# RWKV's A products in tied groups of quadrants, the key's norm as a scale of tokens, and other numbers of streamed products in a hybrid decoder step

## The chip, the cores and the metric

One NeuronCore of a Trainium2 chip runs the whole program. The metric is the device time of one execution in microseconds; lower is better. Engines are named as in the profile: PE is TensorE's matmul, PEld its weight load, DVE VectorE, ACT ScalarE, POOL GpSimd, SP SyncE, which issues most DMAs.

## What is computed

One layer of a hybrid decoder for 512 prompt tokens and 8 x 8 sampled tokens (576 in all), model width 1024, in fp32. RWKV-7 time mixing and differential attention run as two branches on the same normed input, are merged by gates, and a squared-ReLU MLP and a final norm follow. The change is in the RWKV branch. For each of 8 heads of 64, with a per-token decay, a, k, v and r:

```
kk = hs((k * lp['k_k']).astype(f32))
kk = kk / jnp.maximum(jnp.linalg.norm(kk, axis=-1, keepdims=True), 1e-12)
k = k.astype(f32) * (1.0 + (a - 1.0) * lp['k_a'].astype(f32))
S, y = rwkv7_scan(S0, hs(r), hs(decay), hs(k), hs(v), -kk, kk * hs(a))
```

where each step of the scan is

```
sa = jnp.einsum('bhij,bhj->bhi', S, a_t)
S = S * w_t[:, :, None, :] + sa[..., None] * b_t[:, :, None, :] + v_t[..., None] * k_t[:, :, None, :]
return S, jnp.einsum('bhij,bhj->bhi', S, r_t)
```

## The kernel before

The scan is done in chunks of 64 tokens: eight of the prompt, and a ninth that holds the sampled tokens. Activations lie with features on the 128 partitions, so that one tile holds two heads, one on each half; a "head pair" hp is such a tile, four in all (0 to 3), and `halves` names the two halves (par 0 and 1).

`rwkv(hp)` is a generator in stages; `run(...)` near the end calls them in an order that is written out by hand.

- Stage 0 (L753 to L838) makes the operands. The key's squares are summed over each head (pn) and raised to -1/2 on GpSimd (nr, L760). A wide copy on GpSimd repeats each norm over 64 columns (nb, L763), five transposes (pk, pks) turn it round, and VectorE multiplies it into the key (kk, in the buffer sq). The decay's running sum is a scan over tokens (cum, L777), of which ScalarE takes three exponentials (pe, pinv, pm). KB holds a·kk and the scaled key, ST holds -kk and r, each with its decay. The two heads are made by separate instructions on 64 partitions each: in KB head 0 has a·kk first and head 1 second, and ST has one tile per head whose other half is set to zero by GpSimd (L819).
- The A products (pA, L834 on) multiply KB, as weights, by ST for each head and chunk: 18 products of 128 rows and 128 columns a head pair. Because the other half of ST is zero, the sum over 128 rows is that of one head; the 128 outputs are its products with both parts of KB. VectorE masks the results into ABR (own part) and into the free half of ST (other part).
- Stage 1 transposes v (pV, copied into SVU) and KB (pK, copied into KBt) and multiplies the state by ST's ninth chunk (pI).
- Stage 2 solves a triangular system a chunk, in 32x32 blocks: DT is taken from ABR (ScalarE, four pieces), masked into Y and DM, and four rounds of pW, ScalarE's W, pZ, VectorE's update of X and a transpose follow; then pWc and pC fill TT.
- `chain(pr)` walks through the chunks for two head pairs at once with small products (pch), and later stages finish the output.

**What orders the work.** The program is written in Tile, which sorts each engine's instructions by priority and by their readiness as it reckons it; the order is fixed when the program is built, and each engine's queue runs in order. The large products (attention's and RWKV's projections `ps_z`, gates `ps_g`, `ps_brb`) are generators in the list `waiting`. `take(n)` puts out the next n of their matmuls at low priority, so that they fill TensorE between the small dependent steps; `fill(n)` does so behind the last matmul; `blocks` takes nine behind each step of the solve. These are the streamed products: 128 x 128 weights by 288 or 296 columns, in three terms of split fp32. The numbers after each `run` say how many are spent there. PSUM has three rotating banks for this work (`bank`, pool psw), and one more, `tbank`.

`with tc.issue_after(x)` keeps the instructions of a block behind x on its engine. In `chain` a group of products on different quadrants is tied that way to its first one.

Of the kernel before, what the change touches and what calls it, by code (L numbers as in the profile page):

```python
# [41 lines left out]
def tile_hybrid_step(ctx, tc, xT, xsT, ktab, vtab, s0T, ptab, w_in, vecs, w2a2, g2, lamv,  # L42
# [273 lines left out]
    ts(hw0, v(V_W0, 8), 0.5, MUL, 0.0, ADD, GE)  # L316
    ka2 = rc.tile([P, 8], F32, name="ka2")
# [424 lines left out]
    def rwkv(hp):  # L742
# [12 lines left out]
        for t, o in enumerate(toks):  # L755
# [4 lines left out]
        GE.tensor_tensor(out=nr, in0=nr, in1=mhalf[:, :10], op=ALU.pow)  # L760

        nb = rt.tile([P, 5, P], F32, tag="G", name=f"nb{hp}", bufs=3)
        own["nb"] = GE.tensor_copy(out=nb.rearrange("p t (a d) -> p (t a) d", a=2),  # L763
                       in_=nr.rearrange("p (a o) -> p a o", o=1).broadcast_to([P, 10, 64]))
# [16 lines left out]
        VE.tensor_copy(out=pc[:, 0:8], in_=pe[:, 63:NPR:64])  # L781
        VE.tensor_copy(out=pc[:, 8:16], in_=pe[:, NPR + 7::8])
# [5 lines left out]

        kk = sq
# [5 lines left out]
        pk = pks  # L795
        stt(kk[:, NPR:], k[:, NPR:], v(V_KK + hp), pk[:, 64:P], MUL, MUL)

# [14 lines left out]
        stt(aa, aa, 1.0, kk, ADD, MUL)  # L812
        ST = []
        for par, rows in halves:
            stt(KB[rows, :, par], ch(aa)[rows], 0.5, ch(pinv)[rows], MUL, MUL)
            tt(KB[rows, :, 1 - par], ch(k2)[rows], ch(pinv)[rows], MUL)
            st = rb_.tile([P, NCH, 2, 64], F32, tag=f"ST{par}", name=f"ST{par}_{hp}")
            with tc.issue_after(own["nb"].ins) if hp == 0 else nullcontext():
                GE.memset(st[64 - 64 * par:128 - 64 * par], 0.0)  # L819
            stt(st[rows, :, 0], ch(kk)[rows], -1.0, ch(pm)[rows], MUL, MUL)  # L820
            tt(st[rows, :, 1], ch(r)[rows], ch(pe)[rows], MUL)
            ST.append(st)
# [4 lines left out]
        for par in range(2):  # L827
            rows = slice(64 * par, 64 * par + 64)
            oth = slice(64 - 64 * par, 128 - 64 * par)
            for c0, cn, mk in ((0, 4, C_M), (4, 4, C_M), (8, 1, C_MS)):  # L830
                pA = bank(f"pA{hp}{par}{c0}")
                for i in range(cn):
                    mm(pA[:, i * P:(i + 1) * P], KBc[c0 + i], ST[par][:, c0 + i])
                pAv = pA[:, :cn * P].rearrange("p (c w) -> p c w", c=cn)  # L834
                f2 = lambda a: a[:, c0:c0 + cn].rearrange("p c a t -> p c (a t)")
# [690 lines left out]
```

## Time and profile before

| | |
|---|---|
| time, median of 3 runs | 991.74 us (990.62 to 992.3) |
| the profiled execution | 993.35 us |
| its span | 991.6 us |
| TensorE busy | 964.5 us |
| VectorE busy | 694.3 us |
| ScalarE busy | 495.1 us |
| GpSimd busy | 91.0 us |

Times in a timeline count from the span's start. A row of a timeline gives the start, the length, the engine, the line and what is written from what; `x18` means that 18 such records follow each other, and the length goes from the first start to the last end. A matmul of fp32 appears as two records, one of split fp32 (`ps_...`) as one. Ends of matmuls are modelled: records overlap, and the distance of starts is what one costs. Most operations go through helpers, so that a line such as L61 or L72 says only which helper; rows are told apart by tile.

### The profile page before, as it was taken

The page shows a single profiled execution, that of the slowest core. Times are in us where ns is not written, and L with a number is a line of the kernel's source. Part 1 is how long each engine was busy: PE and PEld are TensorE (multiplying, and loading weights), DVE is VectorE, ACT ScalarE, POOL GpSimd, SP SyncE. Part 2 cuts the span into 40 slices and gives each one's busy share as a digit, 9 for nine tenths or more (in the row PEclk, how much of TensorE's full clock was granted, in tenths as well). Part 3 has the DMA queues.
Part 4 walks back from the last instruction along what each step waited for, and adds up shares of the span by engine and source line. Part 5 has one row for each costly group of instructions (what it writes and reads, how often), then busy time and mean ns, then how long its engine had stood idle before and what let it go on. Part 6 is the DMA issues. An engine that isn't in the chain of part 4 may idle for free.

```text
span 991.6 us, 24377 instructions
## 1 busy us (share of the span) xinstructions
PE 964.5 (97%) x9996; PEld 913.4 (92%) x9996; DVE 694.3 (70%) x1459; ACT 495.1 (50%) x1084; POOL 91.0 (9%) x171
## 2 busy tenths in 40 slices
PE   8999999999999998999999999999999999999996
PEld 8999989898986898988889999999999999999996
DVE  6698566874945779445688898966666666666744
ACT  6576455354344455443344767444444444444732
POOL 2611100401003230001200000000000000000001
PEclk9999999999999999999999999999999999999998
DMA  7322673221112215222377642222222222221402
GB/s 266 128 76 76 210 220 117 80 59 52 44 63 74 79 62 161 79 70 100 121 234 223 209 132 97 87 94 86 86 86 86 85 86 86 86 87 42 136 3 95
DMA packets 50832, 105.73 MB, mean 107 GB/s; under 512 B 6066, under 2 KB 8114, under 8 KB 50594
## 3 DMA queue, kind: packets, MB, share of 16 engines
q1 hardware_dynamic: 47442, 96.95, 30.4%
q0 software_dynamic: 1648, 5.35, 1.5%
q8 instruction: 78, 1.28, 0.6%
q10 hardware_dynamic: 1632, 1.89, 0.5%
q14 instruction: 32, 0.26, 0.1%
HBM read 89.38 MB, written 14.78 MB: 105 GB/s over the span
## 4 chain that ended last, share of the span: by engine, by line
PE 83%; DVE 6%; issue 6%; ACT 3%; POOL 1%; DMA 0%; SPq 0%; DVEq 0%; POOLq 0%; ACTq 0%
PE ps_dn L72 21%; PE ps_z L72 8%; PE ps_g L72 7%; PE ux L1250 5%; PE ua L1250 5%; PE ps_wo L72 4%; PE ps_brb L72 3%; PE ps_k L72 3%; PE ub L1250 3%; PE ud L1250 3%; PE ps_bra L72 3%; PE uc L1250 3%; PE pch L1010 2%; PE ps_q L72 2%; PE ps_v L72 2%
## 5 line engine op out<-in xcount | busy, mean ns | idle before, releaser
L72 PE MATMUL ps_dn<-q,hi_dn 128*128 128x288 f32 x768 | 154.7, 296 | 0.0
L72 PEld LDWEIGHTS ps_dn<-q,hi_dn 128*128 128x128 f32 x768 | 122.9, 188 | 1.4
L72 PE MATMUL ps_dn<-q,lo_dn 128*128 128x288 f32 x384 | 113.3, 295 | 0.0
L72 PE MATMUL ps_g<-xl,hi_g 128*128 128x288 f32 x256 | 79.7, 311 | 0.0
L72 PE MATMUL ps_g<-xh,lo_g 128*128 128x288 f32 x256 | 79.2, 309 | 0.0
L72 PE MATMUL ps_g<-xh,hi_g 128*128 128x288 f32 x256 | 78.5, 307 | 0.0
L72 PEld LDWEIGHTS ps_dn<-q,lo_dn 128*128 128x128 f32 x384 | 72.2, 188 | 0.0
L72 PE MATMUL ps_z<-xh,lo_z 128*128 128x288 f32 (+1 forms) x224 | 69.2, 310 | 0.0
L72 PE MATMUL ps_z<-xh,hi_z 128*128 128x288 f32 (+1 forms) x224 | 68.0, 303 | 0.0
L72 PE MATMUL ps_z<-xl,hi_z 128*128 128x288 f32 (+1 forms) x224 | 66.9, 299 | 0.0
L61 DVE TENSOR_TENSOR ya<-ya,ps_dn 128x288 f32<-128x288 f32 x96 | 43.3, 451 | 27.6 <-PE ps_dn L72 27.5
L58 ACT ACTIVATE hi_dn<-raw_dn 128x512 fp32r<-128x512 f32 x48 | 30.1, 628 | 56.2 <-PE ps_dn L72 56.1
L58 ACT ACTIVATE c<-c 128x288 f32<-128x288 f32 x112 | 48.8, 440 | 9.4 <-DVE c L61 7.7
L1250 PE MATMUL ux<-h_t,hi 128*128 128x288 f32 x256 | 52.4, 297 | 0.0
L1250 PE MATMUL ua<-h_b,hi 128*128 128x288 f32 x256 | 52.2, 296 | 0.0
L72 PEld LDWEIGHTS ps_g<-xl,hi_g 128*128 128x128 f32 x256 | 48.9, 191 | 1.5
L72 PEld LDWEIGHTS ps_g<-xh,lo_g 128*128 128x128 f32 x256 | 49.0, 191 | 1.3
L72 PEld LDWEIGHTS ps_g<-xh,hi_g 128*128 128x128 f32 x256 | 48.8, 191 | 1.0
L58 ACT ACTIVATE hi<-a 128x1024 fp32r<-128x1024 f32 (+1 forms) x32 | 27.1, 846 | 43.1 <-PE ps_dn L72 34.9
L61 DVE TENSOR_TENSOR lo<-s,hi 128x1024 fp32r<-128x1024 f32 x32 | 39.2, 1224 | 10.4 <-ACT hi L58 10.3
L72 PE MATMUL ps_dn<-q,w 128*128 128x320 f32 (+1 forms) x336 | 46.3, 298 | 0.0
L72 PEld LDWEIGHTS ps_dn<-q,w 128*128 128x128 f32 x336 | 45.3, 190 | 0.1
(391 smaller groups left out, 2789.1 us busy)
## 6 DMA issues: line engine op xcount, KB each, us to landing
a<-in_w_up_dram SPq DMA_DIRECT2D x32, 512.0 KB, 3.3
raw_dn<-in_w_down_dram SPq DMA_DIRECT2D x64, 256.0 KB, 2.8
raw_g<-in_w_in_dram SPq DMA_DIRECT2D x32, 256.0 KB, 3.0
raw_z<-in_w_in_dram SPq DMA_DIRECT2D x28, 256.0 KB, 3.1
gt_d<-gg SPq DMA_DIRECT2D x16, 288.0 KB, 2.3
g<-gt_d SPq DMA_DIRECT2D x16, 288.0 KB, 3.6
kp<-in_ktab_dram SPq DMA_DIRECT2D x16, 256.0 KB, 4.0
vp<-in_vtab_dram SPq DMA_DIRECT2D x16, 256.0 KB, 3.4
```

The lines of the kernel that those rows point to most:

```text
L58: ring["act"] = AE.activation(out=out, in_=in_, func=func, **kw)
L61: ins = (eng or VE).tensor_tensor(out=out, in0=a, in1=b, op=op)
L72: ring["mm"] = PE.matmul(out=out, lhsT=lhsT, rhs=rhs, start=start, stop=stop)
L1010: ring["mm"] = PE.matmul(out=ps[rows, e], lhsT=lhs, rhs=rhs, start=first and e == 1, stop=True, skip_group_check=True)
L1250: ring["mm"] = PE.matmul(out=ps[:, :288], lhsT=l[:, k], rhs=hb[blk][:, h, k], start=start and i == 0, stop=i == 11, skip_group_check=skip)
```

## The change

- The key's norm is no longer multiplied into the key. KB and ST hold the key without it (with k_k and its sign in `hkk` and `nkk`), and the inverse square of the norm, by VectorE's reciprocal, is brought by six small GpSimd copies into `dn`, one number for each token and head with tokens on partitions. It scales DT ahead of the solve and X behind it. nb, its transposes and kk go.
- KB and ST are made by one instruction for both heads, with a·kk first in both. ST of head 1 is a ScalarE copy of half of head 0's tile; the zeros go.
- Each A product becomes four of 64 rows and 64 columns (`quarter`), one on each quadrant: par chooses the rows, d the part of KB and with it the output's half. d = 0 and d = 1 go to different banks. They are tied in two groups a head pair: chunks 0 to 3 and 8, then chunks 4 to 7. VectorE takes d = 0 for both heads in one instruction into ABR.
- pK is copied to KBt in three pieces a bank instead of one, since the halves must be put back as `chain` wants them.
- The two small columns of decays, pc, come from ScalarE instead of VectorE; pbn uses `tbank`.
- The numbers of `take` around the stages differ; the streamed products are the same in all.

```
+    nkk = rc.tile([P, 4], F32, name="nkk")
+    ts(nkk, v(V_KK, 4), -1.0, MUL, 0.0, ADD, GE)
+    hkk = rc.tile([P, 4], F32, name="hkk")
+    ts(hkk, v(V_KK, 4), 0.5, MUL, 0.0, ADD, GE)
...
         ts(nr, pn[:, 0:10], 1e-24, MAX)
-        GE.tensor_tensor(out=nr, in0=nr, in1=mhalf[:, :10], op=ALU.pow)
-        nb = rt.tile([P, 5, P], F32, tag="G", name=f"nb{hp}", bufs=3)
-        own["nb"] = GE.tensor_copy(out=nb.rearrange("p t (a d) -> p (t a) d", a=2),
-                       in_=nr.rearrange("p (a o) -> p a o", o=1).broadcast_to([P, 10, 64]))
+        VE.reciprocal(out=nr, in_=nr)
+        dn = stat.tile([P, NCH], F32, tag="dn", name=f"dn{hp}", bufs=4)
+        n2 = nr.rearrange("p (t a) -> p t a", a=2)
+        for par, rows in halves:
+            GE.tensor_copy(out=dn[rows, 0:8:2], in_=n2[0:64, 0:4, par])
+            GE.tensor_copy(out=dn[rows, 1:8:2], in_=n2[64:128, 0:4, par])
+            own["nb"] = GE.tensor_copy(out=dn[rows, 8:9], in_=n2[64:128, 4:5, par])
...
-        VE.tensor_copy(out=pc[:, 0:8], in_=pe[:, 63:NPR:64])
-        VE.tensor_copy(out=pc[:, 8:16], in_=pe[:, NPR + 7::8])
+        act(pc[:, 0:8], cum[:, 63:NPR:64], AF.Exp, scale=-KAPPA)
+        act(pc[:, 8:16], cum[:, NPR + 7::8], AF.Exp, scale=-KAPPA)
...
-        pk, pks = bank(f"pk{hp}"), bank(f"pks{hp}")
-        for t in range(4):
-            tr(pk[:, t * P:(t + 1) * P], nb[:, t], ident)
-        tr(pks[:, :P], nb[:, 4], ident)
-        stt(kk[:, :NPR], k[:, :NPR], v(V_KK + hp), pk, MUL, MUL)
...
-            pbn = bank(f"pbn{hp}{t0}")
+            pbn = tbank(f"pbn{hp}{t0}")
...
-        stt(aa, aa, 1.0, kk, ADD, MUL)
-        ST = []
-        for par, rows in halves:
-            stt(KB[rows, :, par], ch(aa)[rows], 0.5, ch(pinv)[rows], MUL, MUL)
-            tt(KB[rows, :, 1 - par], ch(k2)[rows], ch(pinv)[rows], MUL)
...
-            stt(st[rows, :, 0], ch(kk)[rows], -1.0, ch(pm)[rows], MUL, MUL)
-            tt(st[rows, :, 1], ch(r)[rows], ch(pe)[rows], MUL)
+        stt(aa, aa, 1.0, k, ADD, MUL)
+        stt(KB[:, :, 0], ch(aa), hkk[:, hp:hp + 1], ch(pinv), MUL, MUL)
+        tt(KB[:, :, 1], ch(k2), ch(pinv), MUL)
...
+        stt(ST[0][:, :, 0], ch(k), nkk[:, hp:hp + 1], ch(pm), MUL, MUL)
+        tt(ST[0][:, :, 1], ch(r), ch(pe), MUL)
+        act(ST[1][64:128], ST[0][64:128])
...
-            for c0, cn, mk in ((0, 4, C_M), (4, 4, C_M), (8, 1, C_MS)):
-                pA = bank(f"pA{hp}{par}{c0}")
-                for i in range(cn):
-                    mm(pA[:, i * P:(i + 1) * P], KBc[c0 + i], ST[par][:, c0 + i])
...
-                tt(f2(ABR)[rows], pAv[rows], m3(c[rows, mk:mk + P], cn), MUL)
-                tt(f2(ST[par])[oth], pAv[oth], m3(c[oth, mk:mk + P], cn), MUL)
+        def quarter(par, d, ps, at, ci):
+            return mm(ps[halves[par ^ d][1], at:at + P], KB[halves[par][1], ci, d], ST[par][halves[par][1], ci])
...
+        for first, group in ((2, ((0, 4, C_M), (8, 1, C_MS))), (2, ((4, 4, C_M),))):
+            todo, out = [], []
+            for c0, cn, mk in group:
+                ps = [tbank(f"pA{hp}{d}{c0}") if cn == 1 and d == 1 else bank(f"pA{hp}{d}{c0}") for d in range(2)]
+                todo += [(par, d, ps[d], i * P, c0 + i) for i in range(cn) for d in range(2) for par in (1, 0)]
...
+            lead = quarter(*todo.pop(first))
+            with tc.issue_after(lead.ins):
+                for x in todo:
+                    quarter(*x)
+            for c0, cn, mk, x in out:
+                tt(clip(ABR, c0, cn), x[0], m3(c[:, mk:mk + P], cn), MUL)
+            for c0, cn, mk, x in out:
+                for par in range(2):
+                    oth = halves[1 - par][1]
+                    tt(clip(ST[par], c0, cn)[oth], x[1][oth], m3(c[oth, mk:mk + P], cn), MUL)
...
-            act(KBt[:, c0:c0 + cn].rearrange("p c a t -> p (c a t)"), pK[:, :cn * P])
+            act(KBt[:, c0:c0 + cn, 0], pKv[:, :, 0])
+            act(KBt[0:64, c0:c0 + cn, 1], pKv[64:128, :, 1])
+            act(KBt[64:128, c0:c0 + cn, 1], pKv[0:64, :, 1])
...
+        byd = dn.rearrange("p (c o) -> p c o", o=1).broadcast_to([P, NCH, 32])
+        tt(DT, DT, byd, MUL)
...
+            if l == 4:
+                n = NCH
+                tt(X, X, byd, MUL)
...
-    take(221)
+    take(101)
     run(0, 1, 1)
-    take(106)
+    take(146)
...
-    take(190)
+    take(310)
     run(2, 3)
     take(85)
     run(2, 0, 1, 3)
-    take(38)
+    take(18)
```

TensorE's order, at the first head pair's A products. The numbers behind the tile names tell banks and heads apart. Before: pA's 2825, 2832 and 2839 are head 0's three banks, 2843 the first of head 1; ST's 2814 and 2820 are the two heads.

```order
L72 MATMUL ps_z_0_3032<-xl,hi_z_1_3028 128x288
L72 MATMUL pA_2825<-ST_0_2814,KB_2810 128x128 x4
L72 MATMUL pA_2832<-ST_0_2814,KB_2810 128x128 x4
L72 MATMUL pA_2839<-ST_0_2814,KB_2810 128x128
L72 MATMUL ps_z_0_3032<-xh,lo_z_1_3029 128x288
L72 MATMUL ps_z_0_3032<-xh,hi_z_1_3028 128x288
L72 MATMUL ps_z_0_3032<-xl,hi_z_1_3028 128x288
L72 MATMUL ps_z_0_3032<-xh,lo_z_1_3029 128x288
L72 MATMUL pA_2843<-ST_0_2820,KB_2810 128x128 x4
```

Now, from the last quarters of the first group on: 2815 is head 1's ST and 2814 head 0's, 2822 and 2823 the banks of chunk 8 (d = 0 and 1), 2850 and 2851 those of chunks 4 to 7.

```order
L72 MATMUL pA_2821<-ST_0_2815,KB_2810 64x128
L72 MATMUL pA_2821<-ST_0_2814,KB_2810 64x128
L72 MATMUL pA_2822<-ST_0_2815,KB_2810 64x128
L72 MATMUL pA_2822<-ST_0_2814,KB_2810 64x128
L72 MATMUL pA_2823<-ST_0_2815,KB_2810 64x128
L72 MATMUL pA_2823<-ST_0_2814,KB_2810 64x128
L72 MATMUL ps_z_0_3048<-xl,hi_z_0_3040 128x288
L72 MATMUL pA_2851<-ST_0_2815,KB_2810 64x128
L72 MATMUL pA_2851<-ST_0_2814,KB_2810 64x128
L72 MATMUL pA_2851<-ST_0_2815,KB_2810 64x128
L72 MATMUL pA_2850<-ST_0_2815,KB_2810 64x128
```

One streamed product stands between the two groups, where four and three stood between the parts. By the whole order, 49 streamed products now lie between the first head pair's pa and its first pbn, where 74 lay between pk and pbn; and between its last A product and the solve's first step (pW) lie 39, where 137 lay.

VectorE's order, where the first head pair's solve makes its first update of X (from pZ). Before:

```order
L61 TENSOR_TENSOR lo_z_0_3481<-raw_z_0_3476,hi_z_0_3480 128x512
L66 SCALAR_TENSOR_TENSOR P_3230<-Z_3162,mu_204,tz_3228 128x512
L66 SCALAR_TENSOR_TENSOR P_3230<-Z_3162,mu_204,tz_3228 128x8x7
L66 SCALAR_TENSOR_TENSOR P_3230<-Z_3162,mu_204,tz_3228 128x8
L61 TENSOR_TENSOR DM_3_3497<-DT_3266,cst_sb 128x256
L61 TENSOR_TENSOR Z_3234<-ps_z_0_3248,R_108 128x288
L61 TENSOR_TENSOR X_3272<-X_3272,pZ_3328 128x288
L907 STREAM_TRANSPOSE Y_3271<-X_3272 128x288
```

Now:

```order
L69 TENSOR_SCALAR u_3602<-u_3602 128x576
L783 SCALAR_TENSOR_TENSOR cum_3625<-reset,u_3602 128x576
L61 TENSOR_TENSOR DM_3_3323<-DT_3091,cst_sb 128x256
L61 TENSOR_TENSOR Z_3034<-ps_z_1_3049,R_108 128x296
L61 TENSOR_TENSOR ST_1_3652<-P_2958,pe_3627 128x9x64
L61 TENSOR_TENSOR lo_z_0_3464<-raw_z_0_3459,hi_z_0_3463 128x512
L66 SCALAR_TENSOR_TENSOR P_3153<-Z_3034,mu_204,tz_3151 128x512
L66 SCALAR_TENSOR_TENSOR P_3153<-Z_3034,mu_204,tz_3151 128x8x7
L66 SCALAR_TENSOR_TENSOR P_3153<-Z_3034,mu_204,tz_3151 128x8
L61 TENSOR_TENSOR X_3098<-X_3098,pZ_3176 128x288
L61 TENSOR_TENSOR cum_3625<-cum_3625,u_3602 128x576
L918 STREAM_TRANSPOSE Y_3097<-X_3098 128x288
```

The second head pair's u, scan (cum) and ST, which came after the first one's solve, now stand inside it, ahead of and between the updates of X.

More of the change, by code (lines that the diff above doesn't have):

```diff
@@ new lines, in quarter, with clip @@
+        def quarter(par, d, ps, at, ci):
+            return mm(ps[halves[par ^ d][1], at:at + P], KB[halves[par][1], ci, d], ST[par][halves[par][1], ci])
+        def clip(x, c0, cn):
+            return x[:, c0:c0 + cn].rearrange("p c a t -> p c (a t)")
+        for first, group in ((2, ((0, 4, C_M), (8, 1, C_MS))), (2, ((4, 4, C_M),))):
[3 more added lines that the diff above has]
+                todo += [(par, d, ps[d], i * P, c0 + i) for i in range(cn) for d in range(2) for par in (1, 0)]
+                out.append((c0, cn, mk, [x[:, :cn * P].rearrange("p (c w) -> p c w", c=cn) for x in ps]))
+            lead = quarter(*todo.pop(first))
[8 more added lines that the diff above has]
+                    tt(clip(ST[par], c0, cn)[oth], x[1][oth], m3(c[oth, mk:mk + P], cn), MUL)
```

14 lines of the change are left out of this document (2 added, 12 removed).

## The prediction

> **What bounds the kernel now.** I read the page first, then the busy time by stretch, the list of who waited for whom, and the timeline of TensorE around the products that change. The page:
>
> ```profile
> span 991.6 us, 24377 instructions
> ...
> PE 964.5 (97%) x9996; PEld 913.4 (92%) x9996; DVE 694.3 (70%) x1459; ACT 495.1 (50%) x1084; POOL 91.0 (9%) x171
> ...
> PE 83%; DVE 6%; issue 6%; ACT 3%; POOL 1%; DMA 0%; SPq 0%; DVEq 0%; POOLq 0%; ACTq 0%
> ```
>
> TensorE (PE) is busy 97% of the span and holds 83% of the chain that ended last; 27 us of the span are without it. Nothing else is near, so the time after is the time before, less the TensorE time that goes, plus what TensorE newly idles. The change lies in the RWKV stretch, from about 174 to 515 us. Busy time by stretch:
>
> ```profile
> core 0: us, PE busy (x) PEld busy (x) DVE busy (x) ACT busy (x) POOL busy (x), PEclk, DMA share, GB/s
> 174.00:200.00 26.00, 24.42 (x174) 22.89 (x175) 22.09 (x47) 9.04 (x16) 11.76 (x17) 1.00 0.23 76
> ...
> 225.00:250.00 25.00, 24.80 (x623) 22.07 (x612) 11.98 (x23) 11.05 (x23) 4.71 (x11) 0.93 0.15 45
> 250.00:275.00 25.00, 23.25 (x198) 21.73 (x196) 23.71 (x48) 11.21 (x24) 0.10 (x1) 1.00 0.13 44
> ...
> 375.00:400.00 25.00, 22.45 (x439) 19.83 (x441) 24.25 (x45) 11.38 (x25) 0.00 (x0) 1.00 0.54 163
> ```
>
> Where a head pair's operands are made (the first, third and last of these rows) VectorE (DVE) is nearly full too, and TensorE idles most where VectorE is fullest: 2.55 us of 25 in the last row. There VectorE's queue decides when operands come, and the streamed products only cover the wait. The waits of TensorE between 174 and 515 us that the change touches (us in total, times, longest):
>
> ```profile
> PE pk L76 <- POOL nb L763: 2.0, 2, 1.4
> ...
> PE pbn L72 <- DVE rkp L66: 1.5, 2, 1.1
> ...
> PE pI L72 <- ACT KBt L58: 1.0, 2, 0.7
> ```
>
> **The change part by part.** All sums are differences, made against the profiled execution: 993.35 us, a span of 991.6 and 1.75 around it. The median of the three runs is 991.74, 0.16% lower; I carry the difference over to it. A measurement of this kernel can tell about 0.2%, 2 us, from no change.
>
> *The A products.* Now 72 full products, 144 records, since each fp32 product is two. The tile pA, and the timeline of its first nine products:
>
> ```profile
> L72 PE MATMUL pA<-ST,KB x144: 271/276/377, 194.7 to 391.6; 128*128 128x128 f32 x144
> ```
>
> ```profile
> 194.72 2.23 PE L72 MATMUL pA<-ST,KB 128*128 128x128 f32 x18
> ```
>
> The 18 records begin within 2.23 - 0.28 = 1.95 us, 0.115 apart, so the 144 take 16.5 us of TensorE. Afterwards there are 144 products of 64 rows by 64 columns, 288 records, each still with 128 columns of stream, so I let one record keep 0.11 us; what counts is how many run abreast. The nearest rows with small tiles:
>
> ```profile
> 141.63 0.64 PE L72 MATMUL psb<-kp,qbd 128*32 128x128 f32 x16
> ```
>
> ```profile
> 309.20 0.45 PE L1010 MATMUL pch<-R,TT 64*64 64x64 f32 x8
> ```
>
> The 16 records of four column tiles begin within 0.64 - 0.27 = 0.37 us: as four rounds of four that is 0.12 a round, so four run abreast. The eight 64x64 records lie on two opposite quadrants, whose outputs share a bank; they begin within 0.45 - 0.22 = 0.23 us, 0.033 apart, where at half the stream one alone would need 0.055: two run abreast. No row has all four quadrants, which puts two tiles of rows into the same columns. Bounds: four abreast 72 x 0.11 = 7.9 us, two 15.8, none 31.7. I take 7.9, by the row with the same stream.
>
> The Trainium skill (TensorE: Matmul & The Clock Gate, Measured speedup vs the span model) gives a speedup of 10.6 for sixteen tiles, four by four. By an estimate from that page, the same two thirds of four would be 2.65 abreast, 12.0 us, and the sum would end 4.1 us later. The row of four column tiles shows no such loss; no run here shows rows and columns together.
>
> Entering and leaving small tiles costs something:
>
> ```profile
> 281.09 0.29 PE L72 MATMUL ps_g<-xh,lo_g 128*128 128x288 f32 x1
> 281.21 0.29 PE L72 MATMUL ps_g<-xh,hi_g 128*128 128x288 f32 x1
> 281.44 0.82 PE L72 MATMUL pW<-X,DM 32*32 32x32 f32 x72
> 282.19 0.40 PE L72 MATMUL ps_g<-xl,hi_g 128*128 128x288 f32 x1
> 282.43 0.30 PE L72 MATMUL ps_g<-xh,lo_g 128*128 128x288 f32 x1
> ```
>
> Streamed products start 0.12 to 0.13 apart, but 0.23 lies ahead of the first small one and 0.24 behind the first streamed one after it: 0.2 us an excursion. The new order has two groups a head pair, and some are split by other products: ten excursions, 2.0 us. A products together: 7.9 + 2.0 - 16.5 = -6.6 us.
>
> *The key's norm.* Its spread over 64 columns and the 20 transposes of that go:
>
> ```profile
> 181.27 0.66 PE L76 MATMUL pk<-cst_sb,nb 128*128 128x128 f32 x4 [1.44 <-POOL nb L763]
> 181.76 0.27 PE L76 MATMUL pks<-cst_sb,nb 128*128 128x128 f32 x1
> ```
>
> Four start within 0.66 - 0.27 = 0.39 us, the fifth 0.1 later: about 0.11 each, 20 x 0.11 = 2.2 us of TensorE, and the wait of pk, 2.0 us. What is late next there is pbn, the bonus product, with 1.5 us now: at the first head pair 49 streamed products (6.4 us) lie ahead of it, where 74 lay. VectorE has less to do before it, so I leave that wait as it is; between 0 and 4. The norm's new copies are six small ones a head pair on GpSimd, for a scale wanted only in the solve. A power of 2 us leaves that queue with the wide copy:
>
> ```profile
> L760 POOL TENSOR_TENSOR nr<-nr,mhalf x4: 1957/2092/2353, 177.2 to 362.8; 128x10 f32<-128x10 f32 x4
> ```
>
> So I cost the copies at nothing; the cover is the making of the operands, and without it the first solve step would wait for them.
>
> *Vector and scalar work*, from the tiles that the edits write:
>
> ```profile
> L61 DVE TENSOR_TENSOR KB<-k,pinv x8: 740/748/756, 187.3 to 384.0; 64x576 f32<-64x576 f32 x8
> L66 DVE SCALAR_TENSOR_TENSOR KB<-aa,pinv x8: 739/751/756, 188.0 to 382.4; 64x576 f32<-64x576 f32 x8
> ```
>
> ```profile
> L61 DVE TENSOR_TENSOR ABR<-pA,cst_sb x24: 282/681/695, 195.9 to 393.6; 64x512 f32<-64x512 f32 x16, 64x128 f32<-64x128 f32 x8
> L58 ACT ACTIVATE DT<-ABR x16: 438/442/443, 199.1 to 395.4; 32x288 f32<-32x288 f32 x16
> ```
>
> ```profile
> L58 ACT ACTIVATE KBt<-pK x12: 259/592/598, 204.6 to 412.4; 128x512 f32<-128x512 f32 x8, 128x128 f32<-128x128 f32 x4
> ```
>
> ```profile
> L58 ACT ACTIVATE SVU<-pV x24: 198/376/384, 201.6 to 394.8; 64x256 f32<-64x256 f32 x16, 64x64 f32<-64x64 f32 x8
> ```
>
> DT, a quarter of the partitions, still takes 0.44 for 288 columns: time goes with columns. Both heads at once therefore halves KB and, alike in size, ST (from eight instructions of 0.75 a head pair to four, -3.0), halves the eviction into ABR (four of 0.68 and two of 0.28, -1.6), and the product with the norm goes. Two scalings and a reciprocal come, about 1.0. VectorE loses some 4 us a head pair; it does not bound, so I count that only through the waits. ScalarE gets a copy of half of ST and three evictions of a KBt bank for one; it is half idle.
>
> *New waits*, all of TensorE. (a) A group's first part fills all three working banks and the second needs two. They come free after an ABR eviction of 0.68 and the small one of 0.28; one round (0.11) and a streamed product (0.13) cover that: 0.7 us, four times, 2.8. From 0 if the evictions start early, to 1.7 each (6.8) if three other instructions stand ahead of them. (b) pI's bank is freed by three KBt pieces for one; SVU's row has such a piece, 256 columns, at 0.376: 1.1 for 0.592, 0.5 later at the two places where pI waited, 1.0. From 0 to 2.0, all four. (c) At the first head pair 39 streamed products, 5.1 us, stand between the A products and the solve's first step, where 137 stood; pV, pK, pI and the next pair's first products add some 4.6. The chain beneath is one eviction (0.7), ScalarE's six SVU, four DT, nine KBt and four ST pieces (1.9 + 1.8 + 2.9 + 0.8 = 7.4, the last two by size), five vector steps of 0.45 (2.2) and 0.7 of latencies: 11.0, so 1.3 late, from 0 to 2.5. Behind each waiting product stand only streamed ones, in order on the same queue.
>
> Sum: -6.6 - 2.2 - 2.0 + 2.8 + 1.0 + 1.3 = **-5.7 us**; 991.74 - 5.7 = **986.0**. The other numbers of streamed products move the same instructions and remove none: nothing by themselves. The granted clock is 0.93 in the row of 225 to 250: a stretch like it more or less is 1.75 us.
>
> **The rivals.**
>
> *Two abreast, not four.* If two tiles of rows that write the same columns take turns, the A products take 15.8 us and the sum is -5.7 + 7.9 = +2.2: 993.9. For it: no row shows such a pair. Against: both kinds of neighbour, columns alone and opposite quadrants, overlap fully. The Trainium skill (TensorEngine Tiling (Array Packing), Restrictions and Gotchas) says that different row tiles cannot access the same PSUM bank simultaneously. By that rule the two heads, which share each bank here, would take turns. The row at 309.20, two row tiles in one bank, speaks against it.
>
> *Part of the overlap lost.* At 2.65 abreast the products take 288 / 2.65 x 0.11 = 12.0 us, 4.1 more: 990.1.
>
> *Slower: the first solve waits in VectorE's queue.* The making of the second head pair, scan included, now stands between the steps of the first one's solve:
>
> ```profile
> 178.85 0.46 DVE L69 TENSOR_SCALAR u<-u 128x576 f32<-128x576 f32 x1 [2.73 <-ACT u L58]
> 179.34 1.36 DVE L777 TENSOR_TENSOR_SCAN cum<-reset,u 128x576 f32<-128x576 f32 x1
> ```
>
> With these two, some eight of 0.75 and small ones, about 8.1 us stand ahead of the solve's updates of X. If none of it is done early, each is a microsecond of TensorE: 986.0 + 8.1 = 994.1. It ends slower from 5.7 us of waits on. For it: VectorE is busy 95% of the stretch from 250 to 275, which holds the same work now. Against: it needs nothing of the solve and can run while each step's nine streamed products (1.2 us) go by.
>
> **How the numbers follow.** My forecast 0.74, two abreast 0.11, part lost 0.06, slower rival 0.09. The forecast's own bounds: with (a) to (c) at their low ends the sum is -10.8, 980.9; at their high ends (11.3) it is +0.5, 992.2; pbn and the clock widen that by about a microsecond each way. So 980.0 to 993.0, which leaves out about 0.05 below and 0.14 above, most of it the upper halves of two abreast and of the slower rival. Faster by over 0.2% (below 989.8): 0.66 of the forecast, 0.02 of two abreast, 0.02 of part lost, 0.70. Slower by over 0.2% (above 993.7): 0.01, 0.06, 0.01, and 0.07 of the slower rival, 0.15. Within: 0.15.
>
> **What would show it.** pA as 288 records on 64*64, some 2.4 us a head pair with the ends, four starts close together every 0.11 us; starts in twos would mean the first rival. No wait of pk; pA waiting for ABR, about 0.7 four times; pI waiting longer for KBt; the first pair's pW waiting about a microsecond. TensorE's busy time some 9 us lower and its idle time some 3 higher; VectorE near 678 us. I am wrong if TensorE's idle time grows by over 6 us, or its busy time falls by less than 4.

## The result and the profile after

| | before | after |
|---|---|---|
| time, median of 4 runs each | 991.18 us (990.56 to 992.3) | 984.91 us (983.64 to 985.87) |
| ratio, 95% interval | | 0.9929 (0.9912 to 0.9945) |
| the profiled execution, its span | 993.35, 991.6 us | 984.40, 982.6 us |
| mean granted clock of the profiled execution | 0.989 | 0.996 |

The kernel became 0.7% faster, 6.3 us by the medians; 986.0 had been forecast, with 980.0 to 993.0 as its range. The page of the changed kernel:

```profile
span 982.6 us, 24623 instructions
...
PE 951.1 (97%) x10120; PEld 898.2 (91%) x10120; DVE 676.1 (69%) x1427; ACT 507.2 (52%) x1120; POOL 72.8 (7%) x181
```

TensorE's busy time fell by 13.4 us in the two profiled executions and its idle time rose by 4.4 (27.1 to 31.5): 9.0 of span. VectorE's 676.1 is the 678 that was forecast. The same stretches as before, busy time by engine:

```profile
core 0: us, PE busy (x) PEld busy (x) DVE busy (x) ACT busy (x) POOL busy (x), PEclk, DMA share, GB/s
...
174.00:200.00 26.00, 23.59 (x239) 21.11 (x238) 20.51 (x44) 14.64 (x31) 3.78 (x18) 1.00 0.23 73
...
225.00:250.00 25.00, 23.35 (x290) 20.37 (x289) 14.70 (x32) 15.11 (x38) 1.03 (x6) 1.00 0.12 40
250.00:275.00 25.00, 24.86 (x631) 23.17 (x632) 14.20 (x32) 7.63 (x13) 0.20 (x2) 1.00 0.21 67
...
375.00:400.00 25.00, 22.54 (x708) 19.91 (x707) 17.03 (x36) 10.27 (x20) 0.00 (x0) 1.00 0.46 143
```

Two columns matter. VectorE is no longer nearly full (17.03 where 24.25 stood in the last row), and the granted clock is 1.00 in every row of the stage, where before had 0.93 in three.

The A products, as a group and at the first head pair:

```profile
L72 PE MATMUL pA<-ST,KB x288: 269/269/321, 190.3 to 380.6; 64*64 64x128 f32 x144
```

```profile
190.28 1.32 PE L72 MATMUL pA<-ST,KB 64*64 64x128 f32 x40
191.53 0.40 PE L72 MATMUL ps_z<-xl,hi_z 128*128 128x288 f32 x1
192.59 1.29 PE L72 MATMUL pA<-ST,KB 64*64 64x128 f32 x32 [0.65 <-DVE ABR L61]
```

1.32 - 0.27 = 1.05 us lies between the first and the last start of 40 records, ten rounds of four. In the trace four starts stand within 20 ns, and from the second round on each four starts 0.109 us after the last: four quadrants run abreast, and the two first rivals fall. The two heads, on different rows, write the same bank and still start together. The Trainium skill (TensorEngine Tiling (Array Packing), Restrictions and Gotchas) says that different row tiles cannot access the same PSUM bank at once; these records do not agree, where they write different partitions of the bank.

The waits of TensorE between 174 and 515 us that the prediction spoke of:

```profile
PE pW L72 <- DVE X L61: 1.6, 2, 1.2
...
PE pA L72 <- DVE ABR L61: 1.4, 3, 0.7
PE pbn L72 <- DVE rkp L66: 1.4, 2, 0.7
PE pI L72 <- ACT KBt L58: 1.4, 2, 0.8
...
PE ps_g L72 <- DVE gg L61: 1.0, 1, 1.0
PE pK L76 <- ACT SVU L58: 0.7, 1, 0.7
PE pV L76 <- DVE ST L61: 0.7, 2, 0.3
```

pk is gone. The second group of pA waits for ABR and pI waits longer for KBt, as expected. The wait of 1.2 us at pW is not the one that was expected. The first pair's first solve step, at 206.49, does not wait; the second does, at 211 us, for VectorE's update of X:

```profile
206.49 0.82 PE L72 MATMUL pW<-X,DM 32*32 32x32 f32 x72
...
208.65 0.82 PE L72 MATMUL pZ<-W,Y 32*32 32x32 f32 x72
...
212.58 0.41 PE L72 MATMUL pW<-X,DM 32*32 32x32 f32 x26 [1.23 <-DVE X L61]
```

```profile
209.29 0.46 DVE L61 TENSOR_TENSOR Z<-ps_z,R 128x296 f32<-128x296 f32 x1
209.81 0.76 DVE L61 TENSOR_TENSOR ST<-P,pe 128x576 f32<-128x576 f32 x1
210.48 0.68 DVE L61 TENSOR_TENSOR lo_z<-raw_z,hi_z 128x512 fp32r<-128x512 f32 x1
211.09 1.08 DVE L66 SCALAR_TENSOR_TENSOR P<-Z,mu,tz 128x512 f32<-128x512 f32 x3
212.07 0.45 DVE L61 TENSOR_TENSOR X<-X,pZ 128x288 f32<-128x288 f32 x1
```

pZ is done at 209.47, but the update stands on VectorE's queue behind the second pair's ST and pieces of the next projection, and starts at 212.07.

And VectorE's operands, from the groups of the same stretch (total busy time, then mean ns):

```profile
L61 DVE TENSOR_TENSOR ABR<-pA,cst_sb 128x512 f32<-128x512 f32 (+1 forms) x12 | 6.2, 547 | 1.1 <-PE pA L72 1.1
...
L66 DVE SCALAR_TENSOR_TENSOR KB<-aa,hkk,pinv 128x576 f32<-128x576 f32 x4 | 3.2, 808 | 0.0
```

Both heads in one instruction take 808 ns, where one head took 751 and there were two. The 57 ns more are not for the second head: with k_k as a column of a tile (hkk) for the constant 0.5, one head alone takes 810 (the run below with norm and numbers and full products).

For the comparisons below, each of TensorE's records is charged with the time from its start to the next record's start, less idle time. The stretch runs from the first pn to the first ps_bra (174 to 516 us before, 173 to 506 after). In it the A products fall from 15.9 to 11.1 us, the transposes of the norm from 2.1 to 0; idle time grows from 12.8 to 16.3; and before has three stretches of 3.41 us at half clock (from 243.2, 277.4 and 362.7 us), after none. Counting a record's time in these stretches half, an estimate, all other records together take 0.9 us less.

Two executions in a slower state are left out of the medians below: one of the kernel with the norm put back (1035.5 us, mean clock 0.849) and one of before (1824.4 us).

### The profile page after: what moved, and what is told of

Its sections match the earlier page's. It is cut to its first block, busy times and chain, and to the rows that moved or that the text cites. A ratio compares the mean times of both kernels' runs of the same rounds, so it can differ in the third digit from the quotient of the medians.

```text
span 982.6 us, 24623 instructions
## 1 busy us (share of the span) xinstructions
PE 951.1 (97%) x10120; PEld 898.2 (91%) x10120; DVE 676.1 (69%) x1427; ACT 507.2 (52%) x1120; POOL 72.8 (7%) x181
## 4 chain that ended last, share of the span: by engine, by line
PE 56%; DVE 2%; ACT 1%; DMA 1%; issue 1%; POOL 0%; DVEq 0%
PE ps_dn L72 20%; PE ua L1261 5%; PE ux L1261 5%; PE ps_wo L72 4%; PE ps_g L72 4%; PE ps_brb L72 3%; PE ps_bra L72 3%; PE uc L1261 3%; PE ub L1261 3%; PE ud L1261 2%; PE pch L1021 2%; DMA raw_dn<-in_w_down_dram 1%; PE pW L72 1%; PE pZ L72 0%; DVE ya L61 0%
## 5 line engine op out<-in xcount | busy, mean ns | idle before, releaser
L58 ACT ACTIVATE hi<-a 128x1024 fp32r<-128x1024 f32 (+1 forms) x32 | 27.1, 846 | 43.3 <-PE ps_dn L72 34.9
```

The lines of the kernel that those rows point to most:

```text
L58: ring["act"] = AE.activation(out=out, in_=in_, func=func, **kw)
```

## The experiments

Theory A: the gain is work that leaves TensorE, less the new waits, and the numbers of streamed products matter little. Rival B: the gain is the granted clock, that is, half-clock stretches that come or go with the order. After the first four runs a theory C took the place of both in part: the numbers are cover, a piece of streamed work that has to lie at certain places, and the changed operands need it at other places than the old ones.

Each run was timed beside the kernel before on the same chip, four runs to a chip. The medians of before were 992.5 (first four runs), 992.0 (next four) and 991.3 us (last four). The changed kernel itself ran on the first of these chips alone, so a difference between it and a later run carries about a microsecond of doubt.

| run | time, us | ratio to before (95%) |
|---|---|---|
| the changed kernel again | 983.5 | 0.9906 (0.9892 to 0.9921) |
| norm undone | 994.1 | 1.0025 (1.001 to 1.004) |
| quarters in twos | 987.6 | 0.995 (0.9937 to 0.9963) |
| old numbers | 993.0 | 1.0002 (0.9992 to 1.0011) |
| numbers alone | 999.4 | 1.0077 (1.0064 to 1.009) |
| early numbers old | 987.4 | 0.9955 (0.9942 to 0.9968) |
| late numbers old | 988.7 | 0.9963 (0.9949 to 0.9977) |
| norm and numbers, full products | 992.7 | 1.0011 (0.9998 to 1.0023) |
| three more ahead of the first solve | 984.0 | 0.9924 (0.9911 to 0.9938) |
| no cover ahead of pn | 988.6 | 0.9973 (0.9962 to 0.9984) |
| norm and numbers, full products, 25 more ahead | 987.4 | 0.9963 (0.9949 to 0.9978) |
| quarters of one quadrant in a row | 988.6 | 0.9964 (0.9951 to 0.9977) |

### The changed kernel again

No edit.

> The changed kernel once more, as the mark for the next three, and to see the granted clock of many runs of both kernels. Theory A (work): TensorE's time for the A products and the transposes, less the new waits, is the gain; 985, some 6 us below before, whatever clock the runs show. Theory B (clock): before loses three stretches of 3.4 us to a halved clock in the RWKV stage (mean clock 0.989) and the change loses none (0.996), each worth 1.7 us; then before's runs with a mean clock near 0.996 come within 2 us of this kernel, and those near 0.989 lie 7 above it.

983.5 us; the mean granted clock is 0.997 in each of its four executions. The 23 executions of before on the same chip have 0.992 to 0.997, 0.9951 on average. What the clock takes can be estimated from that as the span times what is missing to 1: 4.9 us for before, 2.9 for the changed kernel. So about 2 us of this run's 9.0 are clock, although the profiled executions alone would give it 5. The estimate is good for differences only, and to about a microsecond: both kernels' profiled executions also end with 5 to 8 us at half clock, when TensorE has at most two records left. B falls as the main cause. It expected the executions of before with a clock of 0.996 within 2 us of this kernel; the nine at 0.996 or more take 990.5 to 993.8, at least 7 above it. And the run below with three streamed products more lies 7.3 us under before at nearly the same mean clock (0.994 for 0.995).

### The norm put back

```diff
-        VE.reciprocal(out=nr, in_=nr)
+        GE.tensor_tensor(out=nr, in0=nr, in1=mhalf[:, :10], op=ALU.pow)
...
+        for t in range(4):
+            tr(pk[:, t * P:(t + 1) * P], nb[:, t], ident)
...
-        tt(DT, DT, byd, MUL)
```

> The key's norm goes the old way (power, wide copy, 20 transposes, product with the key); quadrants, both heads at once and the numbers of streamed products stay. Theory A: 20 transposes of 0.11 come back, 2.2 us, and TensorE waits some 2 us for the norm again, less the 1.2 of the first solve step, whose chain loses a scaling: 3 to 4 us slower than the changed kernel, 988 to 989. Theory B: no slower than 2.2 if the mean clock stays at 0.996. A rival that lays the gain to the quadrants alone expects no difference.

994.1 us, 10.6 above the changed kernel where 3 to 4 were expected. Two waits of TensorE make up most of the new idle time:

```profile
PE pk L76 <- POOL nb L766: 2.4, 2, 1.4
PE pbn L72 <- DVE rkp L66: 2.0, 2, 1.6
```

Transposes 2.1 us, idle time 3.2 (19.5 for 16.3; pk's 2.4 and 0.6 more of pbn are most of it), and a mean clock of 0.9937, some 3 us more. These are 8.3 of 10.6; the rest is spread over slightly wider starts and could not be put down to one thing. The numbers of streamed products were kept, so the 10.6 is the price of the norm at a schedule made without it; what is left of it with numbers set for this kernel was not tried.

### Quarters in twos, and those of one quadrant in a row

```diff
-        for first, group in ((2, ((0, 4, C_M), (8, 1, C_MS))), (2, ((4, 4, C_M),))):
+        for first, group in ((0, ((0, 4, C_M), (8, 1, C_MS))), (0, ((4, 4, C_M),))):
...
-                todo += [(par, d, ps[d], i * P, c0 + i) for i in range(cn) for d in range(2) for par in (1, 0)]
+                todo += [(par, d, ps[d], i * P, c0 + i) for d in range(2) for i in range(cn) for par in (1, 0)]
```

For the second kernel the loops are `for d in range(2) for par in (1, 0) for i in range(cn)`.

> The same quarters in another order: d outermost, then chunks, the two heads alternating, so that only two opposite quadrants lie next to each other in the queue. If four abreast is what the products gain from, the 288 records take 0.055 each for 0.027, 15.8 us for 7.9: 7.9 slower, less up to 2 because the banks come free meanwhile: 991 to 993. If overlap does not matter, 985.

> The changed kernel with the quarters ordered so that those of one quadrant follow each other, five or four chunks at a time, instead of four quadrants in turn. If products on one quadrant take turns at 0.11 us a record, the A products take 288 x 0.11 = 31.7 us and some 2 at the ends for 11.1: 984 + 22 = 1006, less a wait for banks of about 1.5: 1004 to 1006. If one quadrant alone streams a record in half that (0.055): 15.8 and the ends, as with two abreast, 987 to 989.

987.6 and 988.6 us: 4.1 and 5.1 above the changed kernel. The first head pair's A products, in twos and then with four of a quadrant in a row:

```profile
191.33 1.81 PE L72 MATMUL pA<-ST,KB 64*64 64x128 f32 x40
193.31 2.32 PE L72 MATMUL pA<-ST,KB 64*64 64x128 f32 x32 [0.17 <-DVE ABR L61]
```

```profile
191.30 5.25 PE L72 MATMUL pA<-ST,KB 64*64 64x128 f32 x72
```

| | A products, us of TensorE | idle time in the stretch, us |
|---|---|---|
| four abreast (the changed kernel) | 11.1 | 16.3 |
| in twos | 16.0 | 14.8 |
| four of one quadrant in a row | 21.1 | 12.8 |

With the order the price does what it should: 5.0 us more in twos. Of the third order 31.7 was expected if products on one quadrant take turns, and 15.8 with the ends if not; 21.1 came, between the two, so that 988.6 lies in the second case's 987 to 989 without being its mechanism. Its first records start one by one, most 0.109 us apart; later ones start together with the next quadrant's, so that the mean is 5.0 / 71 = 0.070. No order here keeps one quadrant alone throughout, and what that costs stays untested. The second column is the lesson: a third of the work that returns is paid out of idle time (1.6 of 5.0, 3.6 of 10.0), because longer A products cover the waits behind them, pA's own above all (1.4 us at four abreast, none in the last order).

### The old numbers, and the new numbers alone

```diff
-    take(101)
+    take(221)
...
-    take(146)
+    take(106)
...
-    take(310)
+    take(190)
...
-    take(18)
+    take(38)
```

> The changed kernel with the old numbers of streamed products (221, 106, 190, 85, 38). Theory A: they move work and remove none, 984 to 987; the first solve step's wait of 1.2 us goes, since 120 more streamed products stand ahead of it. Theory B: the old places of the small products come back, with one to three halved stretches and a mean clock near 0.99: 987 to 990. A rival that lays the gain to the numbers alone expects 991.

993.0 us: the whole gain is gone. This is the run against which A as it stood fails. In its own profile: 3.1 us more idle time than the changed kernel, and three half-clock stretches in the stage; mean clock 0.9926, which takes 7.4 us by the estimate above for 2.9. So of the 9.5 us that the numbers are worth here, B's clock has about 4.5. The largest of the idle time is one wait, at the second head pair's first solve step. TensorE there with the old numbers, and in the changed kernel (some rows between are streamed products):

```profile
258.82 1.32 PE L72 MATMUL pA<-ST,KB 64*64 64x128 f32 x40
...
267.12 1.11 PE L72 MATMUL pI<-ST,s 64*64 64x16 f32 x32 [0.53 <-ACT KBt L58]
...
269.69 0.69 PE L1021 MATMUL pch<-SVU,ST 128*64 128x64 f32 x16
273.20 0.82 PE L72 MATMUL pW<-X,DM 32*32 32x32 f32 x72 [2.83 <-DVE X L894]
```

```profile
240.69 1.11 PE L72 MATMUL pI<-ST,s 64*64 64x16 f32 x32 [0.82 <-ACT KBt L58]
...
259.79 0.82 PE L72 MATMUL pW<-X,DM 32*32 32x32 f32 x72
```

From the first A product until X is ready 273.20 - 258.82 = 14.4 us pass, and only ten streamed products lie between pI and pW to fill the end of them; with the new numbers 133 lie there. The kernel before had none there, and yet its pW waited 0.26:

```profile
260.83 1.05 PE L72 MATMUL pA<-ST,KB 128*128 128x128 f32 x8
...
267.93 1.29 PE L72 MATMUL pA<-ST,KB 128*128 128x128 f32 x10
...
271.39 0.69 PE L1010 MATMUL pch<-SVU,ST 128*64 128x64 f32 x16 [0.42 <-ACT SVU L58]
...
274.43 1.11 PE L72 MATMUL pI<-ST,s 64*64 64x16 f32 x32 [0.68 <-ACT KBt L58]
275.80 0.39 PE L72 MATMUL pW<-X,DM 32*32 32x32 f32 x24 [0.26 <-DVE X L886]
```

Its A products, with 29 streamed ones between them, were drawn out over 8.4 us, so that the evictions began early; of the 15.0 us between the first of them and pW TensorE waited 1.4, in three short waits. From the first A product to pW lie 38 streamed products there and 25 with the changed operands: 13 x 0.13 = 1.7 us less, and the pair's A products are 1.2 us shorter. These 2.9 us are an estimate; the wait grew by 2.6. Packed into two groups, the A products no longer cover the chain that they start. The old numbers had fitted the old products.

If so, the new numbers are wrong for the old operands:

```diff
-    take(221)
+    take(101)
...
-    take(106)
+    take(146)
...
-    take(190)
+    take(310)
...
-    take(38)
+    take(18)
```

in the kernel before.

> Only the numbers of streamed products are the new ones (101, 146, 310, 85, 18); operands, norm and A products are as before, so the output is that of before. Theory 'fitted': the numbers place the next pair's making and the covers for the changed operands; they are worth something only with them. Alone they remove no instruction of TensorE, the waits of pk stay, the second pair's norm and products now fall into the first solve: 990 to 995, no gain against 992. Rival 'numbers by themselves': the 9 us between the changed kernel with old and new numbers come from the order of streamed products whatever the operands are, 3 of them idle time, some 5 half-clock stretches of TensorE: 983 to 985.

999.4 us, 7.4 slower than before and worse than even C had said (990 to 995); the rival by which the numbers give the gain by themselves (983 to 985) falls. The second head pair's first product now follows the first pair's pI with nothing between, and waits 2.3 us for ScalarE's squares; pk's wait stays (2.3).

### The numbers in two halves

```diff
-    take(101)
+    take(221)
...
-    take(146)
+    take(106)
...
-    take(310)
+    take(230)
```

and the other way round, 101, 146, 270, 85, 38.

> The changed kernel with the old first two numbers (221, 106) and a third of 230, so that from the third head pair on the count of streamed products is the new one again. Up to the first pF the order is that of the run with all old numbers, behind it that of the changed kernel. If the loss of the old numbers adds up by place, as that run's profile has it: in the first part 2.0 us more of idle time and two half-clock stretches of 1.7, so 984 + 5.4 = 989.4. If it hangs on the later half alone: 984; if on the earlier alone: 992 to 993.

> The changed kernel with the new first two numbers and the old cumulative counts from the third on (101, 146, 270, 85, 38). If the loss adds up by place: 1.1 us more of idle time and one half-clock stretch in the later half, 984 + 2.8 = 986.8. If it hangs on the later half alone: 992 to 993; if on the earlier alone: 984.

987.4 (expected 989.4) and 988.7 (986.8): 3.9 and 5.2 above the changed kernel, together 9.1, where all old numbers cost 9.5. In the times the loss adds up by place. With the early numbers old, the same wait of 2.8 us at pW is there again, with two half-clock stretches right behind it and a third at 365 us. Idle time is 2.9 us more up to the first pF but 2.5 less behind it, and the mean clock (0.9926) takes 7.3 us by the estimate for 2.9: this half of the loss shows mostly as clock. With the late ones old, there are 1.6 us more idle time behind the first head pairs and one such stretch.

### Norm and numbers without the quadrants

```diff
-            act(KBt[:, c0:c0 + cn, 0], pKv[:, :, 0])
...
+            act(KBt[:, c0:c0 + cn].rearrange("p c a t -> p (c a t)"), pK[:, :cn * P])
...
-                ps = [tbank(f"pA{hp}{d}{c0}") if cn == 1 and d == 1 else bank(f"pA{hp}{d}{c0}") for d in range(2)]
+                pA = bank(f"pA{hp}{par}{c0}")
```

with the operands head by head, as before; then the same with 126 and 121 for 101 and 146.

> The changed kernel but for the A products and the operands: KB and ST made head by head with a zeroed half, 18 full products a head pair, one KBt piece a bank. The norm as a scale of tokens and the new numbers stay. Theory of the prediction: the A products take 15.9 us of TensorE for 11.1, the second group's wait for ABR (1.4) and the wait of pI for KBt go, VectorE's longer making delays the first products of each pair by 1 to 2 us: 984 + 4.8 - 2 + 1.5, that is 987 to 990. Rival: the quadrants give nothing in the end (idle time takes the place of the work) and the norm carries the gain: 983 to 985. Second rival: VectorE's longer making is what counts, 991 and more.

> The run with the norm alone and the new numbers (operands head by head, full A products) with 126 and 121 for 101 and 146, which puts 23 streamed products back between pI and the second pair's pn. Theory: 2.3 us of wait and two half-clock stretches of 1.7 made up most of its 8.7 us over the changed kernel; with the cover they go: 992.7 - 5.7 = 987. What is left over the changed kernel, some 3, is the price of the full products: 16.4 of TensorE for 11.1, less the wait of their second group. Rival: the wait only moves on to the solve, 991 to 993; if the clock doesn't follow the wait: 990.4.

992.7 and 987.4 us. The first is the second rival's number, but not for its reason, VectorE's longer making: the second pair's pn waited for ScalarE's squares (2.3 us) and the clock halved behind it; the stretches of 3.4 us around that wait:

```profile
205.20:208.60 3.40, 1.12 (x24) 1.02 (x20) 2.55 (x7) 2.54 (x7) 0.10 (x1) 1.00 0.09 33
208.60:212.00 3.40, 3.40 (x11) 2.63 (x11) 1.26 (x5) 0.62 (x2) 1.53 (x10) 0.50 0.00 0
```

The second run, at the 987 that was expected, shows it: with 23 streamed products put back ahead of pn the wait is 1.3, and one half-clock stretch follows it instead of two. What remains over the changed kernel, 2.4 to 3.9 us (against 984.9 and 983.5), fits the price of the full products: 16.4 us of TensorE for 11.1, less 3.1 of idle time. The operands made head by head, one KBt piece a bank and the old places of pc and pbn are in this run too, and were not told apart.

### Three streamed products more, and 25 fewer

```diff
-    take(101)
+    take(104)
...
-    take(146)
+    take(143)
```

and 76 with 171.

> The changed kernel with 104 and 143 for 101 and 146: three streamed products (0.4 us) move ahead of the first solve, nothing else is edited. In the order that follows, half of the second pair's gate products (pw, pa) now stand behind the whole first solve instead of ahead of it or within it, so its A products come some 80 streamed products later and only 61 of them are left ahead of the second solve, where 133 stood. Theory 'place': it is the place of the next pair's making, not the count, that the numbers set; the first part then looks as with the old early numbers (there 2 to 3 us more of idle time, two half-clock stretches of 1.7): 986 to 989. Rival 'count': three products more or less change nothing, 983 to 985.

> The changed kernel with 76 and 171 for 101 and 146: the 25 streamed products between pI and the second pair's pn are gone from there and stand behind the second pair's pI. By what the run with the norm alone and the new numbers showed, pn then waits for ScalarE's squares (2.3 us there, where 0 streamed products stood), and two stretches of half clock follow, 1.7 each: the 3.3 us of cover that is taken away shows as idle time less what the wait of the first pW (1.2) gives back, so 984 + 2.3 + 3.4 = 989 to 990. If the clock doesn't follow the wait: 986 to 987. If the wait is covered anyway: 984.

984.0 us for three more: 'place' falls, although half of the second pair's gate products changed sides of the first solve. It left 61 streamed products between the second pI and pW, and they are enough: pI at 251.10, pW at 260.56, no wait. 133, 61 and 10 give 0, 0 and 2.8 us: cover is worth nothing beyond what the chain needs. The wait of 1.2 us behind VectorE's queue is gone as well, since the second pair's u, scan and ST no longer stand ahead of the first solve's X; pA and pbn wait 0.8 us more each, and the time stays.

988.6 us for 25 fewer. TensorE waits for the squares, which stand on ScalarE's queue behind what the first pair still needs:

```profile
PE pn L72 <- ACT sq L58: 3.2, 1, 3.2
```

```profile
199.85 1.46 ACT L58 ACTIVATE KBt<-pK 64x256 f32<-64x256 f32 x5
201.33 0.67 ACT L58 ACTIVATE ST<-pI 64x64 f32<-64x64 f32 x4
202.00 0.89 ACT L58 ACTIVATE DT<-ABR 32x288 f32<-32x288 f32 x2
202.92 0.77 ACT L58 ACTIVATE sq<-P,vec 128x576 f32<-128x576 f32 x1
```

and the stretches of 3.4 us from the wait on:

```profile
200.10:203.50 3.40, 0.49 (x18) 0.39 (x14) 0.47 (x2) 3.28 (x12) 0.00 (x0) 1.00 0.02 5
203.50:206.90 3.40, 3.15 (x12) 2.97 (x13) 2.33 (x7) 0.19 (x1) 0.30 (x2) 0.50 0.00 0
206.90:210.30 3.40, 3.40 (x27) 1.62 (x29) 0.57 (x2) 1.68 (x4) 1.32 (x9) 0.50 0.00 0
```

3.2 us of idle time are followed by two stretches at half clock, in which the time from the start of pn's ten records to the next product is 2.15 us, where it is 1.03 in the changed kernel. The wait of 1.2 us at pW goes in return, and the time is half a microsecond under the 989 to 990 that were expected. The Trainium skill (TensorE: Matmul & The Clock Gate, Part 1: The HAM clock gate (the "warmup" mystery)) has the clock fall to half after an idle window of about 3.4 us; these rows agree, but for the 0.49 us in which TensorE was still busy in the first of them (1.12 in the run with the wait of 2.3).

## Why the prediction was right, and where not

- **What bounds it.** Right: TensorE's work and its idle time make the difference; the granted clock adds to it.
- **A products, -6.6.** Right in mechanism, too large by 1.8: from 15.9 to 11.1 us, -4.8. The rounds cost what was said (72 x 0.109 = 7.9); the old products were 15.9 and not 16.5, and the ends of the groups cost 3.2 and not 2.0.
- **The norm's transposes, -2.2, and the wait of pk, -2.0.** Right: 2.1, and the wait is gone. pbn waits 1.4, where 1.5 was left.
- **New waits, +5.1.** Right in part. pA waits 1.4 for 2.8 (three times, not four, and covered in part), pI 0.4 more for 1.0. The first solve step, priced at 1.3 because 39 streamed products would not cover its chain, waits nothing; its 11.0 us held 0.7 of latencies that no row shows. The 1.2 us that pW does wait come one step later and from VectorE's queue, the slower rival's mechanism at a seventh of its 8.1. That 1.2 stands beside 1.3 is luck.
- **Idle time in all.** The forecast had 5.1 - 2.0 = 3.1 more, and 3.6 came. The waits that it named make only 1.0 of that (3.0 less pk's 2.0). The other 2.6 lie at waits that it did not name, the largest of ps_g for VectorE's gg (1.0), pV (0.7 more) and pK (0.5 more).
- **The sum.** By the records of the two profiled executions, TensorE's work fell by 7.8 us (4.8, 2.1 and the 0.9 of all others) and its idle time rose by 3.6: 4.2 us less, where 5.7 had been forecast.
- **The clock, counted nothing.** It gave about 2 us more: 4.9 us lost before and 2.9 after, by the mean clock of the timed executions. 4.2 + 2.0 = 6.2 is close to the 6.3 of the first comparison; of the 9.0 of the second, 2.8 stay without a place. So the 5.7 came near the time partly by luck: by these estimates the work and the waits gave less, and the clock, which it left out, made up for it.
- **"The other numbers of streamed products move the same instructions and remove none: nothing by themselves."** This step failed. The sum assumed without saying so that cover would lie where the new waits are, and the numbers are what puts it there. With the old ones the kernel is at 993.0, with the new ones alone at 999.4: 9.5 us one way and 7.4 the other hang on a table that removes no instruction. The working did count the streamed products ahead of the first solve, 39 for 137, but priced only what that took away there and not what it gave at the second pair's solve, where ten would have stood.
- **The rivals.** Four starts within 20 ns settle the first two. In twos, the A products cost the 16 us that the rival gave them, and the time is 987.6 and not 993.9, since that is 5.0 us and not 7.9 over four abreast, and idle time pays a third of it. The slower rival, the solve behind VectorE's queue, was there but small: X's first update came late and cost 1.2 us (at 211 us), and the later steps of that solve waited 0.2.
- **TensorE's busy time, "some 9 us lower".** 13.4 in the two profiled executions; 5 of it is the three half-clock stretches that this execution of before had. One profiled execution is a poor measure of them.

With the numbers new, the pieces stand so: neither norm nor quadrants 999.4, the norm alone 992.7, the quadrants (with all that goes with them) alone 994.1, both 983.5 to 984.9. Each is worth more with the other (8 to 11 us for 5 to 7). Not all of that is theirs: the numbers fit the pair, and one count set anew (126) took 5.3 us off the norm alone.

What stays open: why the clock halves where TensorE is not idle. In the kernel before, the stretches ahead of one such place are full:

```profile
236.40:239.80 3.40, 3.40 (x91) 3.14 (x82) 1.32 (x3) 0.96 (x3) 0.00 (x0) 1.00 0.02 5
239.80:243.20 3.40, 3.40 (x82) 3.07 (x80) 0.86 (x2) 2.43 (x7) 1.08 (x1) 1.00 0.30 81
243.20:246.60 3.40, 3.40 (x21) 2.62 (x14) 1.41 (x2) 3.14 (x7) 3.15 (x9) 0.50 0.04 13
```

The stretch ahead of it holds the solve's last 32x32 products and pn's two columns, and fills about a quarter of the array by rows, columns and length of stream (an estimate, against 288 columns in 0.12 us on the whole array). In the traces every half-clock stretch of the RWKV stage stands behind one that is at most a third full by this count. But others as empty are followed by full clock: in the changed kernel one at 483 us (0.13, with an idle wait in it), in the kernel before one at 308 us (0.20, and TensorE busy throughout). A threshold was not found, and no run varied this alone. The rule of the idle window that the Trainium skill gives (TensorE: Matmul & The Clock Gate, Part 1), above, does not reach these rows, in which TensorE is busy throughout. Open, too, is what each smaller part of the change gives: pc on ScalarE, pbn in `tbank` and both heads in one instruction were not undone one by one.

## What to carry to other kernels

When small products are packed closer, the chain that they start loses the cover they gave while they were spread out: move independent work behind them, ahead of the first consumer, and expect to set such counts anew with every change of this kind. Cover beyond what the chain needs buys nothing: 61 products did as well as 133, ten cost 2.8 us of wait and clock beside; how the loss sets in between ten and 61 was not tried. So judge an edit only with its counts refitted. Look also at what a reordered queue of another engine puts ahead of a short dependent step: here it made the one wait that the sum had in the wrong place. Where a wait leaves TensorE idle for two or three microseconds, price it with one or two stretches of 3.4 us at half clock behind it (about 1.7 us each), and take the clock from many executions, not from one profile.

## What the runs showed of the hardware

- Four fp32 products on the four quadrants of 64x64 run abreast at 0.109 us a round of 128 columns, also where two tiles of rows write different partitions of one bank.
- Products on one quadrant start 0.109 us a record apart, but those of the next quadrant start beside the last of them, so that the mean is 0.070 with four of a quadrant in a row.
- VectorE takes the same time for 64 partitions as for 128: 0.75 us for a product of 576 columns, 0.81 with a scaling by a column of a tile beside it.
- A wait of 2.3 to 3.2 us of TensorE at the second pair's pn was followed by two stretches of 3.4 us at half clock in all three runs that had one there; a wait of 1.3 there by one. A wait of 2.8 us at the second pair's pW was followed by one stretch in one run and by two in another.
